# Down product as seven block products, weight sums by adding transfers, no late channel tiles

## The chip, the core and the metric

The kernel runs on one core of a Trainium2 chip. TensorE (PE) multiplies from SBUF into PSUM, VectorE (DVE), ScalarE (ACT) and GpSimd (POOL) work beside it, and SyncE (SP) issues most transfers between DRAM and SBUF; POOL issues some of them too. The metric is the device time of one execution in microseconds. Before the change it is 1815.76 us, the median of three runs (1814.59 to 1818.05). The inputs, outputs and sums are 32-bit floats.

## The reference, cut to the part that changes

The kernel is one layer of a diffusion backbone: input projection, two recurrent mixers, output projection, and then a gated ConvFFN. There are 1152 tokens, 1024 latents and 128 of context, of width 1024, and the FFN has D_FF = 2816 channels.

```python
    h = rmsnorm(x, p['norm_ffn_w']) * (1 + scale2) + shift2
    gt = ffn_conv_fn(h @ p['ffn_w_gate']) + p['ffn_conv_b']
    x = x + gate2 * ((jax.nn.gelu(gt) * (h @ p['ffn_w_up'])) @ p['ffn_w_down'])
    ...
    y_prompt = rmsnorm(xp, final_norm_w)
    y_sample = rmsnorm(xs, final_norm_w)
```

`ffn_conv_fn` is a depthwise 3x3 convolution over the latent grid, and a width-3 one over the context. The change concerns the product with `ffn_w_down` (2816 x 1024) and how the weights of the gate and up products are summed.

## The kernel before

**Arithmetic.** A 32-bit product is made of three matmuls in the type float32r: every operand is split into a high part (ScalarE casts) and a low part (VectorE subtracts), and the products high x high, high x low and low x high are added in PSUM. `split` (L1112) does the two steps. One row tile is 128 tokens, one channel tile 128 channels: 9 row tiles (8 of latents, 1 of context) and 22 channel tiles.

**Order.** The code does not issue instructions as it runs; it records them in a `Plan`. After the last line, `Plan.schedule` deals them out, one engine after the other, in the order of a simulated time with costs written in the code. Among the instructions that are ready it takes the one with the longest chain behind it, plus a lead per function (`LEADS`), plus a nudge (`NUDGE`): one number for each 16 recorded operations of a function. The result is a fixed order on each engine and each queue. `ld` always issues from SP; `st` from POOL or SP, as the planner finds it. A tag (`plan.tag`) is a list of places in SBUF or PSUM that tiles of one kind take in turn; a tile waits until a place is free.

**Front stage** (about 1030 to 1534 us). For each of the 22 channel tiles, `ffn_front` makes the gate and up products for all tokens. It is already a 2x2 block product with seven instead of eight products: token sums stay in SBUF (`hq`, made once by `quarters`), and the weight sums are made for each channel tile in `weights`. There, two transfers of 512 KB bring the gate and up weights, `total` (L2109) makes four sums of 128x512 on VectorE, and `pair` splits each of the seven operands. `product` (L2128) issues 4 x 3 matmuls for each of two token ranges, a of 320 columns and b of 256; `front` (L2168) adds up the results from PSUM, with product 3 behind product 2. `ffn_mid` then convolves (eight VectorE passes over 128x1024, L2225, and two over the context, L2227), applies GELU, multiplies by the up branch and stores the activations in DRAM (`d_a`).

**Late tiles.** `NLATE = 5`: for the last five channel tiles `ffn_mid` is put off. Their gate and up results are stored in `d_gt` and `d_up`, and `late` (L2267) loads them again and runs `ffn_mid` in the down stage.

**Down stage** (1534 to 1809 us). Two halves of eleven channel tiles. In each half `down_weights` loads and splits eleven weight tiles of 128x1024 and keeps them; three row tiles run with the channel tile as the outer loop, the other six with it as the inner loop. `three` (L2282) issues the three matmuls of 512 columns. `finish` takes the first half's result times the gate, adds x and stores it in `d_f`; in the second half it adds the rest, norms and stores the output. `finish_last` does the last row tile in column pieces of 512, 256 and 256.

## Time and profile before

The times below are of one profiled execution: 1818.1 us, of which the profile shows a span of 1816.3 us; the three timed runs have a median of 1815.76 us.

| stage | us | TensorE busy | VectorE busy | GB/s |
|---|---|---|---|---|
| mixers and projections, 0 to 1031.6 | 1031.6 | 984.2 | 826.0 | 173, then 254 |
| front, 1031.6 to 1533.7 | 502.1 | 497.1 | 427.7 | 87 |
| down, 1533.7 to 1809.2 | 275.5 | 275.5 | 169.7 | 180 |
| tail, to 1816.3 | 7.1 | 0.2 | 1.8 | 75 |

The page gives busy times as shares of the span, the chain of work that ended last, and groups of equal instructions with their mean duration and the idle time of their engine ahead of them. A matmul's duration there is its latency; matmuls overlap, so the distance between two starts is what one costs.

### The profile page before, as it was taken

Reading aid. Unit: us, or ns where it says so; the run is one execution under the profiler, and the core shown is the slowest. Engines: PE = TensorE matmul, PEld = TensorE weight load, DVE = VectorE, ACT = ScalarE, POOL = GpSimd, SP = SyncE. Lnnn points to the kernel's source line nnn. Section 1 sums busy time; section 2 is a strip of 40 time slices with the busy share of each in tenths; the row PEclk is TensorE's granted clock in tenths of the full one; section 3 lists DMA queues with packets and bytes.
Section 4 is the critical chain, followed back from the end, with each engine's and each line's share of the span. In section 5 each row is a group of like instructions: output and inputs, shape, how many; then the busy total and the mean of one; then the engine's idle time right before and its main releaser. Section 6 shows DMA issues by size and latency. Waiting matters only on the chain.

```text
span 1816.3 us, 44130 instructions
## 1 busy us (share of the span) xinstructions
PE 1757.0 (97%) x17858; PEld 1570.2 (86%) x17858; DVE 1425.1 (78%) x2689; ACT 868.0 (48%) x1773; POOL 311.7 (17%) x574
## 2 busy tenths in 40 slices
PE   6999999999999999999999999999999999999998
PEld 4899888899988887778778799999999999888887
DVE  6558999987788888876887889999899954868434
ACT  6556766643355555554545754444444333312312
POOL 2014334353322222223211100000000000000000
PEclk9999999999999999999999999999999999999999
DMA  9226547487767688889966522212222247756442
GB/s 323 87 70 171 133 117 179 108 244 198 207 187 234 199 236 259 263 266 284 318 201 233 197 59 74 73 62 85 73 74 73 73 144 239 249 191 206 150 146 86
DMA packets 273100, 307.38 MB, mean 169 GB/s; under 512 B 64019, under 2 KB 217665, under 8 KB 272896
## 3 DMA queue, kind: packets, MB, share of 16 engines
q1 hardware_dynamic: 246608, 224.17, 42.0%
q0 software_dynamic: 26288, 80.40, 13.2%
q8 instruction: 140, 2.29, 0.5%
q14 instruction: 64, 0.52, 0.1%
HBM read 200.50 MB, written 103.99 MB: 168 GB/s over the span
## 4 chain that ended last, share of the span: by engine, by line
PE 84%; DMA 8%; DVE 4%; ACT 2%; issue 1%; POOL 0%; SPq 0%; DVEq 0%; ACTq 0%; POOLq 0%
PE banks L2136 27%; PE banks L1132 7%; PE banks L1134 6%; PE banks L1133 6%; PE banks L2285 5%; PE banks L2286 5%; PE banks L2287 5%; DMA low<-d_ak 2%; PE banks L1784 2%; PE banks L2027 2%; PE banks L2029 2%; PE banks L2028 2%; PE banks L1831 1%; PE banks L1533 1%; PE banks L1370 1%
## 5 line engine op out<-in xcount | busy, mean ns | idle before, releaser
L1132 PE MATMUL banks<-hh,wh 128*128 128x384 f32 x768 | 280.5, 365 | 1.1 <-DVE fx L1321 1.1
L1134 PE MATMUL banks<-hh,wl 128*128 128x384 f32 x768 | 258.5, 337 | 0.0
L1133 PE MATMUL banks<-hl,wh 128*128 128x384 f32 x768 | 258.3, 336 | 0.0
L2225 DVE SCALAR_TENSOR_TENSOR low<-low,pf 128x1024 f32<-128x1024 f32 x176 | 225.3, 1281 | 19.0 <-ACT low L2219 16.7
L2136 PE MATMUL banks<-qm,wh 128*128 128x320 f32 x968 | 223.1, 310 | 0.0
L2136 PE MATMUL banks<-hbm,wh 128*128 128x256 f32 x880 | 163.3, 283 | 1.9 <-ACT fx L2174 1.6
L1132 PEld LDWEIGHTS banks<-hh,wh 128*128 128x128 f32 x768 | 144.9, 189 | 21.7 <-issue 12.8
L2136 PE MATMUL banks<-qm,wl 128*128 128x320 f32 x528 | 162.9, 309 | 0.4 <-DVE wl L2106 0.4
L2136 PEld LDWEIGHTS banks<-qm,wh 128*128 128x128 f32 x968 | 161.0, 189 | 0.1
L1133 PEld LDWEIGHTS banks<-hl,wh 128*128 128x128 f32 x768 | 145.3, 189 | 2.0 <-issue 1.2
L1134 PEld LDWEIGHTS banks<-hh,wl 128*128 128x128 f32 x768 | 144.8, 189 | 0.0
L2136 PEld LDWEIGHTS banks<-hbm,wh 128*128 128x128 f32 x880 | 139.6, 190 | 2.4 <-ACT fx L2174 1.9
L2136 PE MATMUL banks<-ham,wh 128*128 128x256 f32 (+1 forms) x616 | 132.6, 295 | 0.3 <-DVE ham L2069 0.3
L2136 PE MATMUL banks<-hbm,wl 128*128 128x256 f32 x440 | 124.4, 283 | 0.0
L2136 PEld LDWEIGHTS banks<-ham,wh 128*128 128x128 f32 x616 | 102.1, 191 | 0.8 <-DVE ham L2069 0.5
L2136 PEld LDWEIGHTS banks<-qm,wl 128*128 128x128 f32 x528 | 99.1, 188 | 0.7 <-DVE wl L2106 0.7
L2174 ACT COPY fx<-banks 128x320 f32<-128x320 f32 (+1 forms) x132 | 51.8, 397 | 87.2 <-PE banks L2136 80.4
L2106 ACT CAST wh<-fx 128x512 fp32r<-128x512 f32 x88 | 54.2, 619 | 80.8 <-PE banks L2136 66.7
L2285 PE MATMUL banks<-qm,hbm 128*128 128x512 f32 (+1 forms) x221 | 86.4, 391 | 0.0
L2286 PE MATMUL banks<-qm,hbm 128*128 128x512 f32 (+1 forms) x221 | 86.3, 391 | 0.0
L2287 PE MATMUL banks<-qm,hbm 128*128 128x512 f32 (+1 forms) x221 | 86.3, 391 | 0.0
L2136 PEld LDWEIGHTS banks<-hbm,wl 128*128 128x128 f32 x440 | 84.0, 191 | 0.0
(540 smaller groups left out, 4317.9 us busy)
## 6 DMA issues: line engine op xcount, KB each, us to landing
wr<-in_w_in_dram SPq DMA_DIRECT2D x34, 512.0 KB, 4.3
d_a<-low POOLq DMA_DIRECT2D x22, 576.0 KB, 3.1
low<-d_ak SPq DMA_DIRECT2D x64, 192.0 KB, 8.6
low<-in_ffn_w_up_dram SPq DMA_DIRECT2D x22, 512.0 KB, 4.0
wr<-in_ffn_w_gate_dram SPq DMA_DIRECT2D x22, 512.0 KB
low<-d_kb SPq DMA_DIRECT2D x36, 256.0 KB, 3.6
low<-d_a SPq DMA_DIRECT2D x12, 704.0 KB, 4.7
low<-in_ada_w_dram SPq DMA_DIRECT2D x32, 256.0 KB, 5.9
```

The source lines that it names most:

```text
L1132: mm(o, wh[:, kt, :], hh[:, kt, c], kt == 0, False)
L1133: mm(o, wh[:, kt, :], hl[:, kt, c], False, False)
L1134: mm(o, wl[:, kt, :], hh[:, kt, c], False, kt == KT - 1)
L1784: mm(pa[h][:, P * w:P * w + P], kb[hc[h], w, :], W[hc[h], A0[h] + 192 * w:A0[h] + 192 * w + P], True, True)
L2027: mm(ps, oh[:, kt, :], woh, kt == 0, False)
L2106: split(*w, src)
L2136: pe.matmul(o, a[:, kt, :], b[:, kt, :], start=start and first, stop=last, skip_group_check=not start)
L2174: act.copy(keep[n], y[:, 0:w])
L2225: dve.scalar_tensor_tensor(av, shifted(dy, dx), tap(3 * dy + dx), av, MUL, ADD)
L2285: mm(o, lh, w[:, 0, c], first, False)
L2286: mm(o, lh, w[:, 1, c], False, False)
L2287: mm(o, ll, w[:, 0, c], False, last)
```

## The change

**Down product.** The activations are taken as a 2x2 block matrix: latent tokens 0 to 511 and 512 to 1023, channel tiles 0 to 10 and 11 to 21. The down weights are one too: the same channel halves, and output columns 0 to 511 and 512 to 1023. Row tiles i and 4 + i make a pair, four pairs in all. Seven block products of 11 channel tiles and 512 columns take the place of eight; the context tile is computed plainly (`latent`, 22 channel tiles and two column halves). In the program stand 1089 matmuls of this stage against 1221. PSUM holds four banks for one running sum (`dy`) and four for the other (`dz`); sums that are used twice are copied out by ScalarE (`kept`). The token differences (four for each channel tile) are made on VectorE in place; operands are split by halves of 512 columns, in 36 places (`sw`). Weights arrive through four places (`rb`), tokens through seven (`ra`).

**Weight sums.** The four sums of down weights are made in DRAM during the front stage: `down_sums` copies a block to `d_t0` to `d_t3` and adds another by a transfer that accumulates (`acc`, always issued from POOL). The front's own weight sums go the same way: `weights` loads quarters of 256 KB into four places (`fw`) and adds into three of them by `acc`; one sum of four stays on VectorE. In `front`, product 3 goes ahead of product 2.

**No late tiles.** All 22 `ffn_mid` run in the front stage; `d_gt` and `d_up` are gone.

**Orders.** The `NUDGE` table is new for all functions, so every engine's order differs from the first stage on. The planner counts an accumulating transfer's time on the wire 2.1 times (`ADDS`).

```diff
-NLATE = 5
+ADDS = 2.1
-NUDGE = {'step_kernel': [-12, -12, 89, ...
+NUDGE = {'step_kernel': [-74, -18, -9, ...
...
+    def acc(out, src):
+        pool.dma_start(out, src, accum_op=ADD)
...
+    plan.tag("fw", [(plan.tags["wr"].places[0][0], 512 * b) for b in range(2)] + [(low, fru + 512 * b) for b in range(2)], 512)
+    plan.tag("sw", [(qm, 1024 * b) for b in range(14)] + [(ham, 1024 * b) for b in range(8)] +
+             [(hbm, 1024 * b) for b in range(10)] + [(m, 0) for t in ("wh", "wl") for m, _ in plan.tags[t].places], 1024, True)
+    plan.tag("rb", [(plan.tags["wr"].places[0][0], 512 * b) for b in range(2)] + [(low, fru + 512 * b) for b in range(2)], 512)
+    plan.tag("ra", [(fx, 3072), (fx, 3584)] + [(low, 512 * b) for b in range(5)], 512)
...
     def weights(ft):
...
-        yield pair(b11)
-        yield pair(b21)
-        t1 = total(b11, b12)
-        t2 = total(t1, b22)
-        yield pair(t2)
-        yield pair(t1)
-        yield pair(total(b22, b12))
-        yield pair(total(t2, b21))
-        yield pair(b22)
+        t = fetch(b11)
+        yield pair(t)
+        acc(t, b12)
+        yield pair(fetch(b21))
+        r22, t2 = fetch(b22), tl("fw", [P, 4, P])
+        yield pair(t)
+        combine(t2, t, r22, ADD)
+        t3 = fetch(b12)
+        acc(t3, b22)
+        yield pair(t2)
+        acc(t2, b21)
+        yield pair(t3)
+        yield pair(t2)
+        yield pair(r22)
...
+    def down_sums(k):
+        b11, b12, b21, b22 = [down_block(k + HALF * h, n) for h in range(2) for n in range(2)]
+        for j, a, b in ((0, b11, b12), (2, b12, b22), (1, td[0][k], b22), (3, td[1][k], b21)):
+            st(td[j][k], a)
+            acc(td[j][k], b)
...
+        if ft % 2:
+            with plan.behind(len(plan.ops) - 1):
+                down_sums(ft // 2)
...
-        if ft < NFT - NLATE:
-            ffn_mid(ft, raw, us[0])
-        else:
-            st(gtd[ft - NFT + NLATE], raw)
-            st(upd[ft - NFT + NLATE], us[0])
+        ffn_mid(ft, raw, us[0])
...
+    def step(o, a, w, k, fresh):
+        for i in range(4):
+            three(o[i], a, i, w, k == 0, k == HALF - 1, fresh)
...
+    for k in range(HALF):
+        a, w = part(tokens(k, 0)), weight(k, 0)
+        step(ys, a, w, k, True)
+        latent(0, k, c1, k, w)
+        latent(1, k, c1, k, weight(k, 1))
+    c2, b21 = rows_of_context(1), []
+    for k in range(HALF):
+        b21.append(weight(HALF + k, 0))
+        latent(0, k, c2, HALF + k, b21[-1])
+        latent(1, k, c2, HALF + k, weight(HALF + k, 1))
...
+    kept1 = [kept(y) for y in ys]
+    normed(8, cn, [(n, gated(8, n, cn, cz[n])) for n in range(2)])
+    zs = [tl("dz", [P, 512]) for i in range(4)]
+    for k in range(HALF):
+        step(zs, part(tokens(HALF + k, 0)), b21[k], k, True)
+    for i in range(4):
+        f = gated(i, 0, cs[i], zs[i], ADD, kept1[i])
+        st(fd[i][:, halves[0]], f)
+    zs, s3, s4 = [tl("dz", [P, 512]) for i in range(4)], [], []
+    for k in range(HALF):
+        a11, a21, a22, a12 = tokens(k, 0), tokens(k, 1), tokens(HALF + k, 1), tokens(HALF + k, 0)
+        combine(a22, a21, a22, SUB)
+        combine(a21, a11, a21, SUB)
+        combine(a11, a22, a11, SUB)
+        combine(a12, a12, a11, ADD)
+        step(zs, part(a22), total(0, k), k, True)
+        step(ys, part(a11), total(1, k), k, False)
+        s3.append(part(a21))
+        s4.append(part(a12))
+    kept2 = [kept(y) for y in ys]
+    for k in range(HALF):
+        step(ys, s3[k], total(2, k), k, False)
...
+    for k in range(HALF):
+        step(zs, s4[k], weight(HALF + k, 1), k, False)
...
+    last = [(part(tokens(HALF + k, 1)), total(3, k)) for k in range(HALF)]
```

What the planner makes of it is shown at two places. The first is POOL's queue in the front stage. Before, from the last stores of the mixers on (`d_x_117` and `d_h_118` are the residual and normed rows, `d_a` the activations):

```order
L2050 DMA d_h_118<-low 128x1024 x2
L2034 DMA d_x_117<-low 128x1024 x2
L2126 MEMSET low 128x1320
L2235 DMA d_a<-low 128x1152 x16
L2257 DMA d_gt<-low 128x1320
L2258 DMA d_up<-low 128x1152
```

Now, in the middle of the front (L2120, L2126 and L2128 add into `fw` places, whose memory is `low` and `wr`; L2253 copies to and L2254 adds into `d_t0` to `d_t3`, here `d_t_121` to `d_t_124`):

```order
L2253 DMA d_t_121<-in_ffn_w_down_dram 128x512
L2120 DMA low<-in_ffn_w_up_dram 128x4x128
L2254 DMA d_t_121<-in_ffn_w_down_dram 128x512
L2254 DMA d_t_123<-in_ffn_w_down_dram 128x512
L2253 DMA d_t_122<-d_t_121 16x4096
L2128 DMA wr<-in_ffn_w_gate_dram 128x4x128
L2126 DMA low<-in_ffn_w_up_dram 128x4x128
L2254 DMA d_t_122<-in_ffn_w_down_dram 128x512
L2253 DMA d_t_124<-d_t_122 16x4096
L2120 DMA low<-in_ffn_w_up_dram 128x4x128
L2254 DMA d_t_124<-in_ffn_w_down_dram 128x512
L2244 DMA d_a<-low 128x1152
```

Where POOL issued sixteen activation stores in a row and nothing else, it now issues the weight adds of each channel tile between the links of a chain of copies and adds in DRAM.

The second place is VectorE in the down stage. Before, in the first half (L2297 and L2298 gate a row tile and add x, L2367 is the low half of a split of 1408 columns, L2225 and L2234 belong to a late tile):

```order
L2298 TENSOR_TENSOR fx<-banks,fx 128x1024
L2367 TENSOR_TENSOR hbm<-low,hbm 128x1408
L2297 TENSOR_TENSOR banks<-banks,fx 128x1024
L2225 SCALAR_TENSOR_TENSOR low<-low,pf 128x1024 x2
L2234 TENSOR_TENSOR low<-low 128x128
L2225 SCALAR_TENSOR_TENSOR low<-low,pf 128x1024 x3
```

Now, in the pass over the token differences (L2404 to L2407 make them; L2292 is the low half of a split, of tokens from `low` or `fx`, of weights from `wr` or `low`):

```order
L2404 TENSOR_TENSOR low<-fx,low 128x512
L2405 TENSOR_TENSOR fx<-low,fx 128x512
L2292 TENSOR_TENSOR hbm<-low,hbm 128x512
L2292 TENSOR_TENSOR qm<-low,qm 128x512
L2292 TENSOR_TENSOR hbm<-fx,hbm 128x512
L2292 TENSOR_TENSOR ham<-low,ham 128x512
L2292 TENSOR_TENSOR wh_134<-wr,wh_134 128x512
L2406 TENSOR_TENSOR low<-low 128x512
L2292 TENSOR_TENSOR qm<-wr,qm 128x512
L2407 TENSOR_TENSOR low<-low 128x512
```

The convolution passes of the late tiles are gone from this stage; in their place stand short splits and differences of 512 columns, each of which waits for a transfer or for the step ahead of it.

More of the change, by code (lines that the diff above doesn't have):

```diff
@@ L1172, in step_kernel @@
     actd = dram("d_a", [NFT, P, T])
[L1173 to L1174 removed]
     fd = dram("d_f", [NT, P, 1024])
+    td = [dram(f"d_t{j}", [HALF, P, 512]) for j in range(4)]
     dcs = cst("dcs", [P, 2, NCH, 4])
@@ L2284, in three, with part, weight, total @@
+    def part(src):
+        w = tl("sw", [P, 2, 512], F32R)
+        split(w[:, 0], w[:, 1], src)
+        return w
+    def weight(k, n):
+        return part(fetch("rb", down_block(k, n)))
+    def total(j, k):
+        return part(fetch("rb", td[j][k]))
+    def tokens(k, h):
+        return fetch("ra", actd[k][:, 512 * h:512 * h + 512])
+    def three(o, a, i, w, first, last, fresh, c=slice(0, 512)):
+        t = slice(P * i, P * i + P)
         with plan.together():
-            mm(o, lh, w[:, 0, c], first, False)
```

243 lines of the change are left out of this document (117 added, 126 removed).

## The prediction

> **What bounds the kernel now.** I read the page from the top: busy shares, then the chain that ended last, then the stages one by one with the table of windows, then the waits of the engine that bounds.
>
> ```profile
> PE 1757.0 (97%) x17858; PEld 1570.2 (86%) x17858; DVE 1425.1 (78%) x2689; ACT 868.0 (48%) x1773; POOL 311.7 (17%) x574
> PE 84%; DMA 8%; DVE 4%; ACT 2%; issue 1%; POOL 0%; SPq 0%; DVEq 0%; ACTq 0%; POOLq 0%
> ```
>
> TensorE is busy 97% of the span and carries 84% of the chain. An average can hide a stage with another limit, so the stages that the change touches come next: the front stage (gate and up products), the down stage, its tail, and the two parts of everything earlier.
>
> ```profile
> core 0: us, PE busy (x) PEld busy (x) DVE busy (x) ACT busy (x) POOL busy (x), PEclk, DMA share, GB/s
> 0.00:600.00 600.00, 577.00 (x6719) 506.94 (x6720) 480.74 (x1054) 331.70 (x678) 192.07 (x360) 0.99 0.62 173
> 600.00:1031.60 431.60, 407.20 (x6207) 343.10 (x6208) 345.24 (x786) 240.60 (x548) 96.02 (x171) 1.00 0.82 254
> 1031.60:1533.70 502.10, 497.10 (x3713) 495.33 (x3712) 427.67 (x647) 220.47 (x435) 15.47 (x28) 1.00 0.27 87
> 1533.70:1809.20 275.50, 275.50 (x1224) 224.77 (x1222) 169.70 (x198) 73.73 (x110) 8.12 (x16) 1.00 0.54 180
> 1809.20:1816.30 7.10, 0.23 (x2) 0.02 (x1) 1.77 (x5) 1.52 (x4) 0.00 (x0) 0.74 0.20 75
> 1100.00:1300.00 200.00, 200.00 (x1502) 200.00 (x1501) 183.36 (x276) 87.23 (x166) 4.26 (x8) 1.00 0.22 71
> ...
> PE banks L2041 <- ACT low L2007: 2.4, 1, 2.4
> PE banks L2136 <- ACT fx L2174: 1.6, 1, 1.6
> ```
>
> In the down stage PE is busy 275.50 of 275.50 us; in the middle of the front 200.00 of 200.00, beside a VectorE at 183.36 (92%). From 1030 us on PE waits only at the front's very start (the two longest waits stand above). The granted clock is 1.00 in both. So both stages cost what their matmuls cost, and a matmul that goes is a slot that goes, as long as what feeds the rest keeps up.
>
> **The sum: matmuls.** Before, the down stage issues 9 row tiles x 22 channel tiles x 2 halves x 3 = 1188 matmuls of 512 columns; the last tile's three column pieces make them 1155 of 512 and 66 of 256. The changed program has 7 products x 11 x 4 row tiles x 3 = 924, and 22 x 2 x 3 = 132 for the context tile, so 1056; its last tile in two pieces makes that 1023 of 512 and 66 of 256. That is 132 of 512 columns fewer, and the same 66.
>
> ```profile
> 1808.79 0.28 PE L2287 MATMUL banks<-qm,hbm 128*128 128x256 f32 x1
> 1808.91 0.28 PE L2285 MATMUL banks<-hbm 128*128 128x256 f32 x1
> 1780.05 0.23 PE banks L2285
> ```
>
> Two 256-column matmuls start 0.12 us apart, which is their slot (0.28 is latency, overlapped). The chain gives 0.23 for one of 512; finer, (275.5 - 66 x 0.12) / 1155 = 0.232 us. **132 x 0.232 = 30.6 us** go. PE's front stage keeps its matmuls (3696 in both programs).
>
> **VectorE in the front: cover, not gain.** Three of four weight sums per channel tile leave it, five conv passes come back.
>
> ```profile
> L2225 DVE SCALAR_TENSOR_TENSOR low<-low,pf 128x1024 f32<-128x1024 f32 x40 | 51.3, 1283 | 16.9 <-ACT low L2219 16.0
> L2227 DVE SCALAR_TENSOR_TENSOR low<-low,pf 128x128 f32<-128x128 f32 x10 | 3.5, 349 | 0.2
> L2230 DVE TENSOR_TENSOR low<-low 128x512 f32<-128x512 f32 x5 | 3.4, 687 | 0.0
> L2232 DVE TENSOR_TENSOR low<-low 128x512 f32<-128x512 f32 x5 | 3.4, 684 | 0.0
> L2234 DVE TENSOR_TENSOR low<-low 128x128 f32<-128x128 f32 x5 | 1.4, 284 | 0.0
> L2111 DVE TENSOR_TENSOR fx<-fx,low 128x512 f32<-128x512 f32 x9 | 6.2, 689 | 0.2
> ```
>
> One late conv is (51.3 + 3.5 + 3.4 + 3.4 + 1.4) / 5 = 12.6 us of VectorE. A channel tile's PE time is 502.1 / 22 = 22.8 us, VectorE's share of it 0.917 x 22.8 = 20.9; less 3 x 0.689 it is 18.9 us, 83%. All 22 tiles now run so, and the last five no longer leave their 63 us to the down stage. PE ran at 100% beside 92%, so this costs nothing; the store and reload of d_gt and d_up go with it, off PE's path.
>
> **VectorE in the down stage.** It splits 182 operands (before 44, wider), makes 44 token differences, and gates and norms by halves. Nearest rows, for the split at 512 columns and for the gate product out of PSUM:
>
> ```profile
> L2106 DVE TENSOR_TENSOR wl<-fx,wh 128x512 fp32r<-128x512 f32 x36 | 24.5, 688 | 5.2 <-ACT wh L2106 5.1
> L2306 DVE TENSOR_TENSOR banks<-banks,fx 128x512 f32<-128x512 f32 x16 | 11.1, 698 | 37.8 <-PE banks L2287 37.7
> L2312 DVE SCALAR_TENSOR_TENSOR fx<-fx,low 128x1024 f32<-128x1024 f32 x8 | 10.3, 1286 | 0.3
> ```
>
> 182 x 0.688 + 44 x 0.689 + 46 gate steps x 0.69 + 16 x 0.64 + some 6 us of small ones + the last conv's 12.6 = 216 us, of which some 11 stand ahead of the last front product: 205 beside 245 us of PE, 84%. It is uneven: summing both engines along the program's order, the matmul at 147 us of PE's down work needs a VectorE result that has 127 us of VectorE work ahead of it, and the gap stays near 19 us from 107 on. VectorE thus has to keep up at 87% through the first 150 us; the front shows PE whole beside 92%. I take no loss in the middle, and **3 us** at the borders: twice (after the fourth and fifth product) matmuls wait until ScalarE has copied a PSUM bank. Between nothing and 2 x 1.5 us, a copy by the 128x320 row below and a matmul slot or two; I take the upper end, since no row shows this border.
>
> ```profile
> L2174 ACT COPY fx<-banks 128x320 f32<-128x320 f32 (+1 forms) x132 | 51.8, 397 | 87.2 <-PE banks L2136 80.4
> ```
>
> **Adding transfers.** No row shows one. POOL issues 66 into the weight path of the front and 44 in DRAM; the nearest rows are its plain stores, the weight loads of the front and the transfer that lands latest.
>
> ```profile
> d_a<-low POOLq DMA_DIRECT2D x22, 576.0 KB, 3.1
> low<-in_ffn_w_up_dram SPq DMA_DIRECT2D x22, 512.0 KB, 4.0
> low<-d_ak SPq DMA_DIRECT2D x64, 192.0 KB, 8.6
> L2235 POOL DMA_DIRECT2D d_a<-low x22: 533/533/533, 1091.4 to 1674.5; - x22
> L1491 POOL DMA_DIRECT2D d_ak<-top x14: 757/836/868, 137.4 to 384.9; - x14
> ```
>
> An add lands between 3.1 and 8.6 us; I take 5, nearest to the 4.0 of weight loads with the same 512 B pieces, plus a second read. To it come 0.84 for the issue (as d_ak's), 1.4 for the split (VectorE's 0.69 of the L2106 row, as much for ScalarE's cast) and 0.3 that I add for signals. Counted along the built order, 65 adds have at least 7.0 and in the median 11.6 us of PE work (matmuls x 502.1 / 3696) ahead of the first matmul that reads their sum. The need of 7.5 us exceeds that once, by 0.5 us: nothing. With 8.6 it exceeds it 31 times, 39 us in all. Queued behind an add on POOL stand the d_a stores and the DRAM sums, due only in the down stage. The 44 DRAM sums are chains of four stores and four adds per pair of channel tiles, 8 x about 4 us in 45.6 us.
>
> [...]
>
> **Earlier stages.** The new table of nudges deals all orders anew; 8174 matmuls stand ahead of the front in both programs. PE's idle there is 23.0 + 24.4 us by the two windows, so at most 47 can be gained, and a loss has no such bound. I take 0, and a fifth, 9 us either way, for the range.
>
> **The tail** keeps its form (a 256-column piece, gate, square, root, two stores): 7.1 us.
>
> Sum on the profiled execution (1818.1 us, 1816.3 span): 1818.1 - 30.6 + 3 = 1790.5. It lies 2.3 above the runs' median of 1815.76, so **1788** for the median.
>
> **Rivals.**
> *Transfers bind the down stage's first 150 us.* Each 25 us of PE work there carry 20 to 28 loads of 256 KB on SP, 210 to 290 GB/s, against 180 now; 44 weights pass through four places before PE's 61st us, each place held for 4.0 landing + 1.4 split + 0.5 issue: 44 x 5.9 / 4 = 65 us. SP issues in one order, so a load that waits for its place holds the token loads behind it.
>
> ```profile
> 800.00:900.00 100.00, 93.91 (x1566) 78.61 (x1565) 75.89 (x177) 51.12 (x110) 29.41 (x51) 1.00 0.99 297
> 1500.00:1600.00 100.00, 100.00 (x543) 87.57 (x542) 69.09 (x82) 36.53 (x55) 4.26 (x8) 1.00 0.75 254
> ```
>
> At 297 GB/s the engines are full and PE idles 6.1%; at 254 GB/s PE is whole. For: the four places are just enough, landing must not grow. Against: the weights start some 10 us before the front ends, and the pieces (2 KB) are larger than at 800. Price 0.061 x 150 = 9, or (6 us landing: 44 x 7.9 / 4 - 71, the 61 and 10 us of head start) 16 us: 1797 to 1804, and up to 1808 if both come.
>
> *The adds land late* and PE waits in the front: the slower side. Cost by the count along the order: 4 us at a landing of 6.5, 23 at 8, 39 at 8.6, 89 at 10. It eats the net gain of 27.6 from about **8.2 us** on; at 8.6 the time is 1788 + 39 = 1827. For: 8 is the 4.0 of the weight loads doubled, and the d_ak row reaches 8.6. Against: d_ak has small pieces beside full queues (0.82 share), the front's share is 0.27 and at most doubles. [...]
>
> *The orders of the earlier stages* turn out otherwise: 1777 to 1798.
>
> *That it doesn't do what it says* is excluded for the count: 1089 matmuls stand in the built program against 1221.
>
> **Chances.** Forecast 0.56 (1781 to 1796); transfers bind 0.18 (1797 to 1808); adds late 0.14, of which 0.05 still gain (1792 to 1811) and 0.09 end slower; earlier orders 0.12, almost all still faster. The range 1779 to 1809 leaves out some 0.04 below and 0.14 above. Within 0.2% (3.6 us, about what runs of this kernel can tell from no change) lies 0.06, slower 0.12 (the late adds and 0.03 of a bad order), faster 0.82.
>
> **What would show it.** Right: a down stage of about 245 to 250 us between the last front matmul and the tail, PE at 100% in the front, VectorE there near 83%, adds landing under 6 us. Wrong: waits of the front's matmuls for split results behind transfers of the fw tiles; waits of L2310 for splits of rb loads in the down stage; PE idle before 1031 us away from 47.

## The result, and the profile after

The changed kernel takes 1804.2 us (median of six runs, 1802.2 to 1810.1) where the kernel before took 1815.6 beside it: a ratio of 0.9939, 95% interval 0.9922 to 0.9955. The gain is 11.4 us; 27.8 were forecast, and the range (1779 to 1809) holds the time. The profiled execution took 1804.3 us, with a span of 1802.5.

The page after, busy shares and the chain by engine:

```profile
PE 1731.0 (96%) x17726; PEld 1551.9 (86%) x17726; DVE 1455.2 (81%) x2793; ACT 936.1 (52%) x1921; POOL 441.7 (25%) x701
PE 82%; DVE 7%; DMA 6%; issue 2%; ACT 2%; SPq 0%; POOL 0%; DVEq 0%; POOLq 0%; ACTq 0%
```

132 matmuls fewer stand there (17726 against 17858), but TensorE's busy time fell by 26.0 us and the span by 13.8 only. The table of windows after, cut at the first front product (1037.0), the last one (1555.4) and the last matmul; the third and the sixth row are the first and last 25 us of the front:

```profile
0.00:600.00 600.00, 572.05 (x6791) 505.09 (x6792) 478.80 (x1051) 332.13 (x687) 191.01 (x360) 0.99 0.61 169
600.00:1037.00 437.00, 412.98 (x6137) 349.95 (x6136) 346.58 (x783) 243.82 (x547) 94.17 (x174) 0.98 0.81 253
1037.00:1062.00 25.00, 18.48 (x106) 16.72 (x105) 18.17 (x36) 17.43 (x36) 4.49 (x5) 0.86 0.50 118
1100.00:1300.00 200.00, 199.94 (x1501) 199.53 (x1500) 172.91 (x252) 88.24 (x170) 62.74 (x67) 1.00 0.79 164
1300.00:1525.00 225.00, 224.83 (x1687) 224.39 (x1686) 194.40 (x281) 98.06 (x190) 67.33 (x70) 1.00 0.74 151
1530.40:1555.40 25.00, 20.65 (x130) 18.55 (x129) 22.04 (x35) 18.24 (x34) 2.73 (x4) 1.00 0.96 304
1555.40:1795.90 240.50, 238.81 (x1062) 194.82 (x1060) 184.01 (x305) 117.21 (x218) 8.42 (x14) 1.00 0.73 237
```

The first and last 25 us of the front before:

```profile
1031.80:1056.80 25.00, 21.60 (x144) 20.13 (x143) 21.72 (x40) 18.28 (x38) 1.74 (x2) 0.93 0.17 54
1508.70:1533.70 25.00, 25.00 (x190) 25.00 (x189) 12.14 (x19) 10.89 (x21) 1.47 (x3) 1.00 0.79 273
```

Read the second column against the first. The middle of the front is full (199.94 of 200.00) and the down stage nearly so (238.81 of 240.50). What is lost lies at the edges: the front starts 5.2 us later, TensorE idles 6.5 us in the front's first 25 (3.4 before) at a clock of 0.86 (0.93), and 4.4 us in its last 25 (none before), where VectorE is busy 22.04 us instead of 12.14. The waits of TensorE after 1025 us (line, engine and line waited for, us, times, longest):

```profile
PE banks L2145 <- DVE wl L2115: 2.9, 4, 2.3
PE banks L2145 <- ACT wh L2115: 2.4, 1, 2.4
PE banks L2047 <- ACT low L2013: 2.1, 2, 1.4
PE banks L2310 <- ACT low L2202: 1.7, 1, 1.7
PE banks L2145 <- DVE low L2013: 1.5, 1, 1.5
PE banks L2310 <- ACT banks L2441: 0.6, 1, 0.6
PE banks L2145 <- ACT fx L2183: 0.5, 2, 0.4
PE banks L2310 <- DVE banks L2439: 0.5, 1, 0.5
PE banks L2310 <- DVE low L2440: 0.5, 1, 0.5
```

Both kernels from the first front product to the last matmul: 777.4 us before, 758.7 after, so 18.7 fewer.

### The profile page after: what moved, and what is told of

It reads as the page before. It is cut to its first block, busy times and chain, and to the rows that moved or that the text cites. A ratio compares the mean times of both kernels' runs of the same rounds, so it can differ in the third digit from the quotient of the medians.

```text
span 1802.5 us, 44849 instructions
## 1 busy us (share of the span) xinstructions
PE 1731.0 (96%) x17726; PEld 1551.9 (86%) x17726; DVE 1455.2 (81%) x2793; ACT 936.1 (52%) x1921; POOL 441.7 (25%) x701
## 4 chain that ended last, share of the span: by engine, by line
PE 82%; DVE 7%; DMA 6%; issue 2%; ACT 2%; SPq 0%; POOL 0%; DVEq 0%; POOLq 0%; ACTq 0%
PE banks L2145 25%; PE banks L2310 14%; PE banks L1139 7%; PE banks L1141 6%; PE banks L1140 6%; PE banks L1790 2%; DMA fx<-d_y 1%; PE banks L2033 1%; PE banks L2034 1%; PE banks L2035 1%; PE banks L1837 1%; PE banks L1659 1%; PE banks L1844 1%; PE banks L1861 1%; DMA d_kb<-top 1%
## 5 line engine op out<-in xcount | busy, mean ns | idle before, releaser
L2234 DVE SCALAR_TENSOR_TENSOR low<-low,pf 128x1024 f32<-128x1024 f32 x176 | 225.0, 1280 | 9.5 <-ACT low L2228 6.9
L2183 ACT COPY fx<-banks 128x256 f32<-128x256 f32 (+1 forms) x132 | 52.3, 398 | 143.5 <-PE banks L2145 142.4
L2115 ACT CAST wh<-low 128x512 fp32r<-128x512 f32 x88 | 54.4, 619 | 57.7 <-DMA low<-in_ffn_w_up_dram 32.4
L2145 PE MATMUL banks<-ham,wl 128*128 128x256 f32 (+1 forms) x264 | 77.1, 292 | 0.0
L2115 DVE TENSOR_TENSOR wl<-low,wh 128x512 fp32r<-128x512 f32 x88 | 60.3, 687 | 16.5 <-ACT wh L2115 16.1
L2254 POOL DMA_DIRECT2D d_t<-in_ffn_w_down_dram x44 | 43.0, 1093 | 86.5 <-DMA d_t<-d_t 42.2
```

What stands on the lines that cost most here:

```text
L2115: split(*w, src)
L2145: pe.matmul(o, a[:, kt, :], b[:, kt, :], start=start and first, stop=last, skip_group_check=not start)
L2183: act.copy(keep[n], y[:, 0:w])
L2234: dve.scalar_tensor_tensor(av, shifted(dy, dx), tap(3 * dy + dx), av, MUL, ADD)
L2254: acc(td[j][k], b)
```

## The experiments

All ratios are to the kernel before, run beside each on the same chip. Its own median was 1815.6 to 1821.4 us in these batches, so the ratios compare better than the times. The last three columns come from each run's profile: when the first front product starts, the time from there to the last matmul, and TensorE's idle time (window less busy) in the front's first 25 us / its middle / its last 25 us / the down stage.

| run | median us | ratio (95%) | front starts | front + down | idle |
|---|---|---|---|---|---|
| before | 1815.6 | | 1031.8 | 777.4 | 3.4 / 1.6 / 0.0 / 0.1 |
| changed | 1804.2 | 0.9939 (0.9922 to 0.9955) | 1037.0 | 758.7 | 6.5 / 0.5 / 4.4 / 1.7 |
| e1_early_order | 1797.4 | 0.9879 (0.9854 to 0.9903) | 1028.3 | 758.9 | 6.7 / 0.5 / 2.3 / 1.7 |
| p0_same_again | 1797.2 | 0.9872 (0.9850 to 0.9894) | 1035.0 | 760.8 | 7.4 / 0.7 / 2.8 / 1.7 |
| x1_before_new_order | 1826.2 | 1.0038 (1.0024 to 1.0053) | 1036.0 | 778.8 | 4.9 / 0.0 / 0.0 / 0.8 |
| e2_first_sums_dve | 1802.4 | 0.9912 (0.9888 to 0.9937) | 1033.1 | 759.6 | 9.6 / 0.5 / 3.4 / 1.7 |
| x3_own_order_first_dve | 1812.8 | 0.9961 (0.9948 to 0.9975) | 1039.6 | 764.6 | 6.0 / 5.3 / 3.1 / 1.7 |
| e4_front_sums_dve | 1836.8 | 1.0111 (1.0076 to 1.0146) | 1028.2 | 797.0 | 9.6 / 23.2 / 2.1 / 3.2 |
| e5_no_dram_sums | 1799.9 | 0.9901 (0.9872 to 0.9929) | 1028.9 | 762.6 | 7.1 / 4.7 / 0.8 / 2.3 |
| e3_sums_earlier | 1804.4 | 0.9926 (0.9905 to 0.9948) | 1028.9 | 765.4 | 7.1 / 4.5 / 2.8 / 1.8 |
| x4_product_twice | 1851.7 | 1.0177 (1.0153 to 1.0200) | 1025.2 | 800.0 | 7.1 / 0.9 / 5.5 / 7.6 |
| p4_product_twice | 1834.3 | 1.0083 (1.0058 to 1.0108) | 1037.3 | 792.7 | 6.7 / 2.0 / 2.6 / 1.8 |
| p1_norm_first | 1796.7 | 0.9883 (0.9861 to 0.9906) | 1028.6 | 757.3 | 5.8 / 0.8 / 3.1 / 2.3 |
| p2_norm_and_split | 1800.8 | 0.9901 (0.9880 to 0.9922) | 1033.4 | 756.8 | 5.9 / 0.8 / 3.7 / 1.8 |
| p3_after_norm_split | 1806.3 | 0.9932 (0.9914 to 0.9950) | 1037.1 | 760.5 | 6.0 / 0.5 / 3.4 / 1.7 |
| p5_conv_behind | 1803.1 | 0.9914 (0.9890 to 0.9939) | 1029.1 | 762.9 | 5.9 / 0.5 / 8.1 / 1.7 |
| p6_conv_behind2 | 1805.7 | 0.9923 (0.9900 to 0.9946) | 1035.1 | 762.7 | 5.4 / 0.5 / 8.5 / 1.7 |
| p7_no_dram_sums | 1800.5 | 0.9899 (0.9880 to 0.9917) | 1031.4 | 760.6 | 7.2 / 0.5 / 2.9 / 1.7 |

### The order of the early stages

Theory: the newly dealt order ahead of the front costs about 5 us by itself. Rivals: chance, or the new transfers reaching back. Those operations are the same in both kernels, so the order of before can be written into the changed kernel:

```diff
             def rank(x):
                 op = x[0]
+                if op.id < len(PIN):
+                    return (1e6 if self.ENGINES.index(e) == PIN[op.id] % 8 else -1e6) - PIN[op.id] // 8
```

> The changed kernel, but every instruction ahead of the front is dealt in exactly the order of the kernel before. In the profile after, the first front product starts at 1036.8 us where it started at 1031.6 before. If the re-dealt early order costs that, the front starts near 1031.6 again and the time falls by about 5 us to 1799. If the 5 us are a variation of the granted clock or of the execution, the front starts anywhere from 1031 to 1037 and the median stays within 2 us of 1804. If the extra transfers reach back into the early stages (the first adding transfers are issued before the first front product), it stays at 1036 to 1037 with the old order as well.

Measured: 1797.4 us, 6.7 under the changed kernel; by the ratios it is 0.0060, some 11 us, and the two intervals do not touch. Front and down stage take the same time to 0.2 us, though their order at the front's start and from the border on was dealt anew. The reverse puts the changed kernel's early order into the kernel before (by the traces the orders on VectorE, ScalarE and POOL agree to 968 us and differ in single places from there to the front):

> The kernel before, unchanged in what it computes and in its front and down stage, but its instructions ahead of the front are dealt in the changed kernel's order. The changed kernel gained 6.7 us in its median (1804.2 to 1797.4) when it got the early order of before. If that order is what costs, and the new matter of the change has no part in it, the kernel before gets slower by 5 to 8 us (1821 to 1824 beside 1815.6), and its first front product starts at about 1037. If the early order only costs together with the adding transfers or the new weight loads, it stays within 2 us of 1815.6.

Measured: ratio 1.0038, slower by 6.9 us, front and down stage unchanged (778.8). A second run of e1's program:

> The instructions of the run with the early order of before (1797.4 us, ratio 0.9879 with 0.9854 to 0.9903) once more, in the same order, as a base on this chip and as a second profile of it. The kernels that share its early order started the front anywhere from 1025 to 1037 us in their profiles. If that is chance from one execution to the next, this one starts it somewhere else than at 1028.3, while front and down stage together (758.9 us) come out within 1.5 us.

The ratio repeats (0.9872). Its profile tells what a single profile is worth here: the same instructions in the same order start the front at 1035.0 instead of 1028.3.

```profile
600.00:1028.30 428.30, 406.29 (x6180) 341.89 (x6167) 340.82 (x777) 237.80 (x541) 96.69 (x170) 0.99 0.82 254
600.00:1035.00 435.00, 412.15 (x6253) 347.44 (x6246) 345.41 (x792) 240.25 (x547) 97.43 (x174) 0.98 0.81 253
```

So one profile's early part is uncertain by some 7 us, and the verdict rests on the timed runs. Two pairs of kernels differ in little but the early order: changed and e1 by 0.0060 of the ratio (11 us, plus or minus 5), x1 and before by 0.0038 (7 us, plus or minus 3). Two more pairs point the same way (x3 and e2: 0.0049; p3 and p2, whose two edits are alike: 0.0031), but in their profiles front and down stage differ too, by 5.0 and 3.7 us, so they say little of the early order. The profiles agree in the mean: the front starts at 1037.4 in the four kernels with the new order (1036.0 to 1039.6) and at 1031.0 in the fourteen with the old one (1025.2 to 1037.3). Which instructions of it cost is not known.

### What the 132 matmuls are worth

> The early order of before, and one of the seven products of the down stage run a second time on the same operands (132 more matmuls of 512 columns, no further loads, sums or splits; that block of the output then holds the product twice). If the 132 matmuls which the change takes out are worth what the prediction took (132 x 0.232 = 30.6 us), the time rises by 30 to 31 us over 1797.4, to 1828. If the seven-product stage is held by transfers or by VectorE, part of the added work is hidden in waits and it rises by less than 25 us.

```diff
-        step(ys, s3[k], total(2, k), k, False)
+        w = total(2, k)
+        step(ys, s3[k], w, k, False)
+        step(ys, s3[k], w, 1, False)
```

It rose by 54 us (0.0298 of the ratio). But the scheduler had dealt the whole program anew around the added matmuls: the span behind the last matmul grew from 7 to 17 us, and TensorE's idle time by 10. The nudges were made for another list of operations, and this is the likely price of losing them. So from here on the complete order of e1 was written down, instruction by instruction on each engine, and only single entries of it were moved or added:

```diff
-            cand = [x for x in ready[e] if x[1] <= t + 1e-9]
-            x = max(cand, key=rank)
+            x = next(x for x in ready[e] if x[0].id == line[e][0])
```

> The second run of one product (132 more matmuls of 512 columns, that block of the output holds it twice), this time with every other instruction in exactly the order of the run with the early order of before, so that nothing else is dealt anew: in the earlier try the scheduler also dealt the rest of the kernel differently, its last matmul left a tail of 17 us instead of 7, and TensorE's idle time grew by 10 us. If 132 matmuls are worth 30.6 us, the time rises to 1828 (ratio 1.0050 to 1.0060, where it was 0.9879). If the seven products run with cover that the eighth would use, it rises by less than 25 us; if it rises by 40 us and more, a matmul of the dense stage costs more than the median row of the profile, and the work term of the prediction is wrong.

By the timed runs it rose by 0.0204 of the ratio, 37 us, plus or minus 6. The down stage itself, between the last front product and the last matmul, without and with the added product:

```profile
1548.10:1787.40 239.30, 237.61 (x1056) 193.59 (x1054) 183.97 (x303) 116.10 (x218) 7.70 (x13) 1.00 0.73 238
1558.70:1830.30 271.60, 269.84 (x1189) 219.83 (x1187) 184.78 (x304) 115.76 (x218) 7.68 (x13) 0.99 0.64 209
```

It is 32.3 us longer with the same idle time, against p0's 240.8 it is 30.8: 0.233 to 0.245 us a matmul. The price of 0.232 stands by the profiles, and nothing hid the added work; the 37 us of the timed runs lie 6 above it, at the edge of their uncertainty. Of the 42.7 us between the two profiles' spans (1836.9 and 1794.2) 9.0 lie ahead of the front, within what p0 showed for chance or little beyond it.

### Adding transfers or VectorE

Three runs made weight sums on VectorE again, those of tile 0 (e2 and x3, the other 21 keep the adds) or all (e4, whose diff this is):

```diff
...
-        acc(t, b12)
...
-        acc(t3, b22)
...
-        acc(t2, b21)
...
+        t1 = both(r11, r12)
+        t2 = both(t1, r22)
...
+        yield pair(both(r22, r12))
+        yield pair(both(t2, r21))
...
```

> The early order of before, and the weight sums of channel tile 0 alone made on VectorE again, the other ten tiles' by adding transfers. If the adding transfers land late where channel tile 0 runs its seven products behind one another on a half-filled front, TensorE's idle time in the first 24 us of the front (6.4 us after, 3.4 us before) falls back to about 3.4, and the time is 3 to 4 us below the run with the early order alone. Rival: the idle time there is VectorE's cast and split of low weights, and the sums only add to VectorE's queue: no change, or 1 to 2 us slower.

> The changed kernel with its own early order kept, and only the weight sums of channel tile 0 made on VectorE. In the profile after, VectorE sat idle 3.25 us and ScalarE 2.03 us until the first adding transfer of the front landed at 1042.4, with the last tile's normalization queued behind both. If that wait is what costs at the front's start, the idle time of TensorE in its first 25 us falls from 6.5 to about 4 and the time by 2 to 4 us to 1800 to 1802. If the place of the normalization in the two queues is what costs, whatever stands ahead of it, it stays at 6 to 10 us as in the other run with these sums on VectorE (9.6), and the time is 1804 or more.

> The early order of before, and all weight sums of the front on VectorE (no adding transfer in the weight path; the sums of the down weights stay adding transfers in DRAM). If the adding transfers cost only at the front's start and border, the middle of the front stays at 100% TensorE with VectorE at 91 to 93% instead of 86 to 87%, and the time equals the run with only tile 0 on VectorE within 2 us. If VectorE had been near binding, as the kernel's makers of the sums by transfer would suppose, waits of 3 us and more on VectorE come up in the middle of the front and it is slower than that run by as much. If the adds were what costs at the border, TensorE's idle there falls from 4.6 to about 2.

None helped. With tile 0 alone on VectorE the front's first 25 us idle 9.6 us (e2), or the middle idles 5.3 (x3); with all tiles the middle idles 23.2, and the kernel is slower than the one before. The middle of e4:

```profile
1100.00:1300.00 200.00, 191.35 (x1407) 188.76 (x1406) 174.52 (x257) 80.98 (x159) 23.25 (x34) 0.99 0.43 109
```

VectorE is busy 174.52 us there, less than the 183.36 beside which TensorE was whole before. So a full VectorE is not what e4 shows, but VectorE's place in the order may be: from 1025 us on TensorE waits 13.8 us for VectorE's splits (seven waits, the longest 4.2), the sign that was named for a VectorE near its limit. Like x4 it was dealt anew without nudges of its own, so load and order can't be told apart. At the front's start no run without the adds of tile 0 idled less than 6.0 us (6.5 with them). What the adds are worth against VectorE in a tuned order stays open.

### The front's start

In the changed kernel the sum that waits for the first add stands on VectorE ahead of the last attention tile's normalization (L1149, L1151), on which the token quarters depend:

```profile
1039.06 0.15 DVE L1149 TENSOR_SCALAR low<-low 128x1 f32<-128x1 f32 x1
1042.45 0.69 DVE L2124 TENSOR_TENSOR wr<-low,wr 128x512 f32<-128x512 f32 x1 [3.25 <-DMA low<-in_ffn_w_up_dram]
1043.06 0.15 DVE L1149 TENSOR_SCALAR low<-low 128x1 f32<-128x1 f32 x1
1043.73 0.15 DVE L1151 RECIPROCAL low<-low 128x1 f32<-128x1 f32 x1
```

In e1's order other work stands ahead of it. Moved in both (here VectorE's part in e1):

```diff
 L2197 TENSOR_TENSOR low<-banks,fx 128x4x64
+L1156 RECIPROCAL low<-low 128x1 x2
 L2120 TENSOR_TENSOR wl_136<-low,wh_134 128x512
 ...
-L1156 RECIPROCAL low<-low 128x1
 L2080 TENSOR_TENSOR hbm<-fx,hbm 128x4x128
-L1156 RECIPROCAL low<-low 128x1
```

> Every instruction in the order of the run with the early order of before (1797.4 us, ratio 0.988 to the kernel before), but six are moved at the start of the front: the two reciprocals of the last attention tiles' normalization ahead of two splits of weights on VectorE, and on ScalarE their two square roots ahead of one cast of weights and their two scalings (2.19 us) ahead of the casts of the token quarters. In that run the reciprocals were issued at 1036.8 and 1037.5 though the square roots were done at 1033.1, and TensorE sat idle 6.7 us in the front's first 25 with its clock at 0.73. If the normalization's place in the two queues is what costs at the front's start, the idle time falls to 3 to 4 us, the clock rises to about 0.9, and the time falls by 4 to 7 us (ratio 0.984 to 0.986). If the front waits there for the adding transfers or for VectorE's whole load, the idle time only moves to the next wait and the time stays within 1.5 us.

> The changed kernel in its own order throughout, but for the same two edits: the normalization (two reciprocals on VectorE; two square roots and two scalings on ScalarE) goes ahead of the sum and the cast that wait for the first adding transfer to land (VectorE idle 3.25 us and ScalarE 2.03 us at 1042.4), and at the border the split goes ahead of three convolution passes. No transfer is moved. If the adding transfer's late landing costs through what is queued behind it, TensorE's idle time in the first 25 us falls from 6.5 to about 4, at the border from 4.4 to about 2, and the time from 1804.2 to 1798 to 1800 (ratio 0.990 to 0.992 where it was 0.9939). If the adding transfers themselves are waited for, nothing falls by more than 1 us.

The first product on the last quarter, in e1 and in p1 (whose fronts start 0.3 us apart):

```profile
1046.89 0.80 PE L2150 MATMUL banks<-hbm,wh 128*128 128x256 f32 x2 [2.67 <-ACT low L2018]
```

```profile
1044.39 0.80 PE L2150 MATMUL banks<-hbm,wh 128*128 128x256 f32 x2 [2.95 <-ACT low L2018]
```

The product starts 2.5 us earlier (2.8 counted from each front's start), but TensorE waits for its next link (2.95 us) and idles 0.9 us less. Front and down stage are 1.6 us shorter than in e1's profile; the times are the same (0.9883 against 0.9879 and 0.9872). p3 is the same for the changed kernel: 0.9932 against 0.9939. Both fall under the rival: the wait moves.

### The border of front and down stage

In the changed kernel and in e1 the front's last weight split but two stands behind four convolution passes (changed kernel, VectorE, then TensorE):

```profile
1527.78 5.24 DVE L2234 SCALAR_TENSOR_TENSOR low<-low,pf 128x1024 f32<-128x1024 f32 x4
1532.93 0.69 DVE L2115 TENSOR_TENSOR wl<-low,wh 128x512 fp32r<-128x512 f32 x1
```

```profile
1533.68 0.42 PE L2145 MATMUL banks<-qm,wl 128*128 128x320 f32 x1 [2.30 <-DVE wl L2115]
```

That is 2.3 of the changed kernel's 4.4 us there. Another 1.7 stand before the down stage's first products (L2310 <- ACT low L2202 above): they wait for a copy out of a bank, which ScalarE issued behind a cast that had waited 1.15 us for the load of a down weight. e1 has no such wait.

Two theories: VectorE's load (no late tiles), or the sums in DRAM at POOL's queue and on the transfer engines. First the sums, moved earlier or left out, with the rest dealt anew:

> The early order of before, and the eleven groups of sums of down weights in DRAM dealt at earlier channel tiles, so that the last is done by channel tile 16 of 22 rather than 21. Without any DRAM sums TensorE sat idle 0.8 us in the last 25 us of the front, with them 2.3. If what costs there is the sums that stand late in GpSimd's queue, the idle time falls to about 1 us and the time is 1 to 2.5 us below 1797.4, the run with the early order alone. If the border waits for the loads of the down weights themselves, which all kernels have, it stays at 2.3 us and the time within 1 us; and if denser sums hold up the weight adds in the middle of the front, TensorE's idle time there rises from 0.5 us and the kernel gets slower by as much.

> The early order of before, and no sums of the down weights in DRAM: in their place the down stage loads single blocks of the weight (the sums are left out, so the output is not the reference's), while the front's own adding transfers stay. If the chain of DRAM sums at the head of GpSimd's queue holds back the last weight add of the front, TensorE's idle time at the border of front and down stage (4.6 us after) falls to about 2, and the time is 2 to 3 us below the run with the early order alone. If the border's wait is VectorE's and ScalarE's own order there, it stays at 4 to 5 us and the time within 1 us. The middle of the front and the down stage are full in both theories and stay within 1 us.

```diff
-        if ft % 2:
-            with plan.behind(len(plan.ops) - 1):
-                down_sums(ft // 2)
...
-        return part(fetch("rb", td[j][k]))
+        return part(fetch("rb", down_block(k, 0)))
```

(The diff is that of e5; e3 calls `down_sums` at eleven earlier tiles.) The border's idle time fell to 0.8 us without the sums and stayed at 2.8 with earlier ones, and both lost 4 us in the middle: new orders again. With e1's order kept:

> The run with the early order of before (1797.2 and 1797.4 us in two tries) with the 88 instructions of the DRAM sums left out and every other instruction in its place; the down stage loads single blocks instead of sums, so the sums are left out of the output. In the border of that run TensorE is idle 2.3 to 3.0 us, 2.3 of it on one split behind four convolution passes. If the DRAM sums, at GpSimd's queue or on the transfer engines, hold the border, the idle time falls to about 1 us and the time by 2 us or more; if VectorE's queue holds it, it stays at 2.3 to 3.0 us and the time within 1.5 us of 1797.

```profile
1528.78 0.42 PE L2150 MATMUL banks<-qm,wl 128*128 128x320 f32 x1 [2.30 <-DVE wl L2120]
```

The same wait on the same split, and no gain in time. **The sums in DRAM cost nothing here that these runs can tell**; e5's better border came from its order. Then VectorE's side, one step after the other:

> As the run before, and one more instruction moved: at the front's end the split of the last channel tile's third weight sum goes ahead of three convolution passes (1.31 us each) on VectorE, behind four of which it was issued at 1525.5 although its cast was done at 1521.0; TensorE waited 2.30 us for it. If that queue place is what costs at the border, the idle time of the front's last 25 us falls from 2.3 to below 0.5 us and the time by another 2 to 4 us. If the late DRAM sums and loads hold the border, the wait moves to the next weight and the time stays within 1 us.

> As the run with the normalization and one split moved ahead (1800.8 us, ratio 0.990), and at the front's end the remaining three convolution passes of the last but one channel tile on VectorE (3.9 us in sum), with the two steps that follow them on VectorE and ScalarE, go behind the front's last three additions and weight splits. There the wait of TensorE had only moved from the split (2.3 us) to an addition that frees a bank, queued behind the same passes (2.0 us), and the idle time of the front's last 25 us was 3.7 us. VectorE was busy 22 to 23 of 25 us there, where it was 12 in the kernel before, which left five channel tiles' middle part for the down stage. If VectorE's load of channel tiles that are no longer late is what costs at the border, the idle time falls to 1 to 1.5 us and front and down stage together from 757 to 754 or 755 us. If the loads of the down weights and the DRAM sums hold it, it stays at 3 us or more.

> The run with three convolution passes behind the front's last additions made a new wait of 8.1 us: the activation that follows the passes stood on ScalarE ahead of the copy that frees a bank for the front's last products. Here that activation goes behind this copy, the two multiplications after it behind one more split, and the rest is as there. If VectorE's load at the border is what costs, the idle time of the front's last 25 us now falls to 1 to 1.5 us (3.0 to 3.7 in the runs without the move) and front and down stage together to 754 to 756 us. If it stays at 3 us or more with the wait on a load or on the split of a down weight, the transfers hold the border.

```diff
 L2239 SCALAR_TENSOR_TENSOR low<-low,pf 128x1024
 L2120 TENSOR_TENSOR wl_135<-low,wh_133 128x512
-L2239 SCALAR_TENSOR_TENSOR low<-low,pf 128x1024 x3
 L2209 TENSOR_TENSOR low<-banks,fx 128x320
 L2209 TENSOR_TENSOR low<-banks,fx 128x256
+L2120 TENSOR_TENSOR wl_136<-wr,wh_134 128x512 x2
+L2239 SCALAR_TENSOR_TENSOR low<-low,pf 128x1024 x3
```

p2 took the 2.30 us away, and an addition behind the passes took its place with 2.0 (2.75 in p3). With all passes behind (p6), TensorE waits 7.51 us for a copy out of a bank on ScalarE, and ScalarE stood at a cast of the down stage's tokens, whose load was late:

```profile
1541.73 0.64 PE L2150 MATMUL banks<-qm,wh 128*128 128x320 f32 x1 [7.51 <-ACT fx L2188]
```

```profile
1538.10 0.51 ACT L2372 CAST ham<-low 128x384 fp32r<-128x384 f32 x1 [5.80 <-DMA low<-d_a]
```

That load was late because of VectorE, not of other transfers. The down stage's tokens (`ra`) take places in `low` where the last channel tiles' gate results (`graw0`, `graw1`) lie, so SP holds the load until the convolution passes of the last but one tile have read them, and SP issues in one order: every load behind it waits too. In p6 the passes end at 1535.38, the load goes out at 1535.45, and the cast starts at 1538.10. The longest waits of SP's queue at the border, in the changed kernel and in p6:

```profile
SPq L2365 <- DVE low L2234: 9.2, 1, 9.2
```

```profile
SPq L2370 <- DVE low L2239: 14.9, 1, 14.9
```

In the changed kernel the load goes out at 1533.08, when the four passes above end (1533.02). p5 and p6 pushed three of the passes behind, and with them all of SP's loads (14.9 us in both): they made the border worse, and so are no evidence against VectorE's load. The sums are ruled out (p7). What the rows show is the passes of a tile that is no longer late, ahead of a split, of an addition and of the loads. Not shown is how much of the border they cost in all: in e5 and e1 SP waits the same 9.2 us, and TensorE idles 0.8 and 2.3. A run with late tiles in the changed kernel was not tried.

## Why the prediction was wrong

The table sets each step of the prediction against the profiles of before and after (1816.3 to 1802.5, so -13.8 us).

| step | predicted | measured |
|---|---|---|
| matmuls | -30.6 | -26.7 as what is left of front + down, an estimated 1.1 of the gap is the clock at the front's start |
| copies of banks in the down stage | +3 | 0: no such wait on the page |
| front's middle | 0 | -1.1 idle |
| front's start | 0 | +3.1 idle |
| front's end | 0 | +4.4 idle |
| down stage's end | 0 | +1.6 idle |
| earlier stages | 0, 9 either way | +5.2 (7 and 11 by the timed runs) |
| tail | 0 | -0.3 |

- **Matmuls.** Right in count and price (p4). Of the gap of 3.9 us, an estimated 1.1 is the lower clock in the front's first 25 us (0.86 and 0.93: 18.48 x 0.14 less 21.60 x 0.07); 2.8 stay unassigned.
- **"Earlier stages: I take 0".** This is the step that failed most, and the one that runs show. The new order costs 7 us in the kernel before (x1) and 11 in the changed one (e1); with the old order the gain is 22 to 23 us by the ratios, of 27.8 forecast. The 0 had no row behind it; the bound of 9 lies between the two figures. The sign named for it came too: TensorE idles 52.0 us ahead of the front, against 47.4, though one profile settles little here (p0). The traces count 12925 matmul instructions there in both programs, not 8174; that they are equal is what the step needed.
- **"All 22 tiles now run so ... so this costs nothing".** This is the second step that failed, by 4.4 us of idle time at the front's end. A share over the whole front (83% forecast, 86% measured in its middle) says nothing of its end, where the front's last split and the down stage's loads now meet convolution passes. VectorE is busy 88% of the last 25 us; with the late tiles it was 49% and TensorE whole. The rows show 2.3 us of it as a wait for a split behind the passes. That late tiles would free this border again is argued from them, not shown by a run; three ways of moving VectorE's work there (p2, p5, p6) and taking the DRAM sums out (p7) did not.
- **The borders that were priced** (3 us for the bank copies) cost nothing, and VectorE was busy 184.0 of the down stage's 240.5 us, where 205 beside 245 were forecast. Those that cost 9.1 us of idle time (3.1, 4.4 and 1.6 in the table) were not on the list. How much of the 3.1 at the front's start is the change's own is open: x1, the kernel before with the new order and no adds, idles 4.9 there in its profile. The last 1.6 us are plain in the chain: the last tile's two column pieces share a bank, and TensorE waits for VectorE twice and ScalarE once in turn (0.5, 0.5 and 0.6 us).
- **Adding transfers.** Their need was taken as 7.5 us. In it, the second read added to a weight load's 4.0 and the 0.3 for signals are the author's estimates, as is the doubling of the 4.0 to 8 for late adds: no run shows them as such. What the runs show is the issue and the landing. In the changed kernel, three lines of adds (the issue on POOL in ns, minimum, median, maximum; the landing, for L2126, in us):

```profile
L2126 POOL DMA_DIRECT2D low<-in_ffn_w_up_dram x22: 1264/1337/1889, 1046.9 to 1521.4; - x22
DMA to landing us min/median/max: 4.7/6.1/7.9
...
L2120 POOL DMA_DIRECT2D low<-in_ffn_w_up_dram x22: 1276/1334/1362, 1035.2 to 1513.4; - x22
...
L2254 POOL DMA_DIRECT2D d_t<-in_ffn_w_down_dram x44: 805/863/2279, 1104.9 to 1576.9; - x44
```

  The issue takes 1.34 us instead of 0.84 and the landing 4.9 to 6.1 by line (medians) instead of 5, so the need is up to 9.1 with the split and signals. The prediction's count put 4 us on a landing of 6.5. In the middle of the front, TensorE still waits only 0.23 us in 425 (199.94 of 200.00 and 224.83 of 225.00): the count of work ahead was the right argument and had room. That held although another premise failed: the transfer engines' share in the front "at most doubles" from 0.27, the prediction said, and it rose to 0.79 and 0.74 (0.22 in the middle before). At the front's start there is no such room, and the first add held two queues (3.25 us on VectorE).
- **The rival that transfers bind the down stage** fell: from 1550 to 1775 us TensorE is whole at 280 and 245 GB/s. (Its two prices together, 9 and 16 us, would have made 1813, not the 1808 of the prediction.) What came of it is its remark that a load waiting for its place holds those behind it, at the border ahead of the stage.

```profile
1550.00:1575.00 25.00, 25.00 (x120) 20.90 (x119) 22.61 (x33) 13.74 (x22) 3.52 (x5) 1.00 0.93 280
1575.00:1775.00 200.00, 200.00 (x867) 162.51 (x866) 156.35 (x259) 105.58 (x196) 5.75 (x10) 1.00 0.74 245
```

- **POOL's issue of an add** took longer than the nearest row, 1.34 us against 0.84, but within 1276 to 1362 ns for all 22 adds of L2120, beside a VectorE at 86%, which looks like a fixed price rather than a wait. Other lines have longer issues too (up to 1889 ns for L2126, 2279 for L2254), and what those waited for is not shown.

The changed kernel with the early order of before (1797.4 and 1797.2 us in two tries, ratios 0.9879 and 0.9872) is faster than both kernels; none of the other moves bettered it measurably.

## What to carry to other kernels

Work that leaves a full stage is worth its slots (31 to 32 us for 132 matmuls in p4), but look for the loss at the stage's first and last 25 us, each engine by itself, the loading queue too: work that is put off may be what keeps such a border free, and work that still reads a place holds the loads that want it (SP waited 9.2 us in the changed kernel, 14.9 in p6). Where a table of tuned numbers sets the order, changing the list of operations changes everything that the table does, also far from the change; price that as a term of its own. To test one cause in such a kernel, write down the complete order and move single entries; a kernel dealt anew answers another question.

## What the runs showed of the hardware

At the front's start, where TensorE waits, the granted clock fell: in stretches of 5 us to 0.70 from 1045 us on in the kernel before, to 0.70 and 0.67 from 1045 and 1055 on in the changed one, and to 0.50 in e1. So more is lost there than the idle time. In e1, behind waits of 2.08 and 1.10 us:

```profile
1035.00:1040.00 5.00, 2.92 (x18) 2.66 (x17) 3.51 (x10) 4.18 (x6) 2.63 (x2) 0.89 0.66 96
1040.00:1045.00 5.00, 2.94 (x12) 1.74 (x10) 3.77 (x9) 3.56 (x8) 0.00 (x0) 0.50 0.26 33
1045.00:1050.00 5.00, 3.11 (x14) 3.11 (x15) 5.00 (x10) 4.50 (x10) 0.00 (x0) 0.50 0.00 0
```

At half clock the 6 us of matmuls in the last two rows are some 3 us of work, an estimate from the 0.50: there the clock cost about as much as the idle time ahead of it. Three matmuls of 256 columns took 0.64 us from 1047.70 on, and 0.36 from 1052.70 on. Between the first two waits TensorE ran nothing but eight transposes, in 1.92 us (1.03 us from 1016.57 on, at a clock of 1.00); the longest wait of this stretch, 2.67 us, came later, ahead of 1046.89. What lowered the clock is not shown.

At the border it was not the length of the wait alone. The 5 us behind the same wait of 2.30 us there, amid matmuls alone, in the changed kernel and in e1:

```profile
1533.68:1538.68 5.00, 5.00 (x37) 5.00 (x38) 5.00 (x10) 4.80 (x9) 0.00 (x0) 1.00 0.76 243
```

```profile
1526.24:1531.24 5.00, 5.00 (x25) 5.00 (x26) 5.00 (x10) 4.59 (x9) 0.00 (x0) 0.66 0.79 252
```

At a clock of 0.66 TensorE got through 25 matmuls where it got through 37 at 1.00, so a busy share of 5.00 in 5.00 hides some 1.6 us (an estimate: 12 of 37 matmuls). In stretches of 5 us around and behind the same wait the clock fell to 0.66 in p4, 0.72 in p7 and 0.82 in p0, and stayed at 1.00 in p1; what decides is not shown.

An adding transfer of 256 KB in 512 B pieces took 1.34 us of POOL to issue, one in 2 KB pieces into DRAM 0.86 us.
